# Two gate chunks of a fused encoder layer computed as a block product, and attention A's transposes and values one step later

## The chip, the cores and the metric

The kernel runs on one core of one Trainium2 chip. The metric is the device time of one execution in microseconds (us). A core has five engines with a queue each: TensorE (PE in the profile; its weight loads are shown as PEld), VectorE (DVE), ScalarE (ACT), GpSimd (POOL) and SyncE (SP), which here only issues transfers. Transfers run on 16 DMA engines that all queues share. An engine works through its queue in order, and waits there until what the next instruction needs is ready.

## The reference

One layer of an encoder is applied to two sequences, of 256 and 1024 rows of 1024 numbers, in float32. The kernel treats them as one matrix of T = 1280 rows, in three column blocks of 512, 512 and 256 when it is transposed.

```python
h = _rmsnorm(x, g_mix)
z = h @ w_in                      # queries, keys, values of branches A and B, and 2 x 1024 gates
...
gates = jax.nn.sigmoid((z[..., o6:] + b_gate).astype(jnp.float32)).astype(x.dtype)
gates = gates.reshape(b, S, 2, D_MODEL)
o_a, _ = _banded_attention(qa, ka, va, A_WINDOW, 1, rel_bias[:, :A_HEADS], sink)
o_b = _dilated_mixture(qb, kb, vb, rel_bias[:, A_HEADS:])
merged = gates[:, :, 0] * (o_a.reshape(b, S, A_Q) @ w_branch_a) + gates[:, :, 1] * (o_b @ w_branch_b)
x = x + merged @ w_out
h = _rmsnorm(x, g_mlp)
return x + jnp.square(jax.nn.relu(h @ w_up)) @ w_down
```

Attention A has 8 heads of 64 with 2 key heads, a window of 128 rows to either side, a bias by distance and a sink. Branch B has three groups of 4 heads, with windows that skip rows; their results are mixed by softmax weights. A final norm ends the layer.

## The kernel before

Every float32 matrix product is three matmuls on a rounded high part and the remainder (`mm3`, `six`): low by high, high by low, high by high. ScalarE makes the high part, VectorE the remainder.

**The input projection** produces 128 columns of z at a time, a *chunk*. The 16 gate chunks are c = 0 to 15. Most chunks are computed two at a time by `pair`, as a 2 x 2 block product of the 1024 long rows with seven block multiplications in place of eight (`seven`, each 12 matmuls of 512 columns), and two ordinary products for the 256 short rows (`prompt`, each 24 matmuls of 256 columns). `PAIRS` lists the pairs. The first `MIXED` of them run alone; beside the last five runs attention B (`attention_b`), advanced by a `tick`. The gates of a pair go to DRAM, `scr_g`, at once.

**Attention A** follows. `PLAIN` lists the gate chunks that no pair has; the generator `logits` computes them in the ordinary way (per chunk 48 matmuls of 512 columns and 24 of 256), as a *filler* that is advanced a few matmuls at a time: a group is four matmuls of 512 columns or eight of 256. A chunk has 15 groups. When a block is finished, ScalarE copies it to "gs", and SP stores it to `scr_g`.

A's main loop goes over n = 40 units of work, `order[j]` = (u, t), for u in 4 pairs of heads and t in 10 row tiles, two of them in one step (j = 0, 2, ..., 38). A step issues, in this order: the values of the step before last, the transposes of the last step, the scores of its own two tiles with filler between and behind them, their exponentials, two pieces of `merge` (which combines the three groups of B on POOL, with loads on SP), and loads that are due. `scores` takes two PSUM banks "sc", which VectorE frees when it has added the bias into the tile "s". `transposes` turns "s" in PSUM ("pt" and one "mm" bank) and copies it out with ScalarE and VectorE. `values_of` multiplies by v, copies to "o" on VectorE and stores it to `scr_o` on SP. A step transposes up to 12 blocks of 128 x 128, in three groups of four: the first and third group are copied by ScalarE, the second by VectorE. `values_of` needs all three.

**The gate jobs** come last: 24 for branch b, 24 for branch a. Job i multiplies a weight by a merged attention output, and VectorE multiplies the result by the opened gate into mT. Gates are loaded by `load_gate` (two gates share a slot "sg"), opened by a sigmoid in `open_gate` two jobs ahead, and requested eight jobs ahead. Before and beside the jobs the attention outputs are split in two parts: `high_b` and `low_b` for branch B, `turn_a` and `low_a` for A, after A's outputs have been divided by their row sums. The row sums are finished in `sums_a`, turned and written to DRAM in `rows_a`, and loaded back, spread over partitions, by `widen` ("wl").

From the first attention on, every engine's instructions stay in the order in which the program issues them. Tiles come from pools with a fixed number of slots: `slot` (33 of 4 KB per partition), `wslot` (10), `qslot` (8 of 1 KB), the attention pool (`a3`), and eight PSUM banks ("mm" 3, "sc" 2, "pt" 2, "pv" 1). A new tile waits until a slot of its pool is free.

Of the kernel before, what the change touches and what calls it, by code (L numbers as in the profile page):

```python
# [15 lines left out]
P = 128  # L16
# [30 lines left out]
PAIRS += [(0, P), (2 * P, 3 * P), (512, OFF_G)] + [(OFF_G + P * c, OFF_G + P * c + P) for c in (1, 3, 5, 7, 9)]  # L47

MIXED = 9
PLAIN = range(11, 16)  # L50
# [47 lines left out]
def encoder_kernel(  # L98
# [1046 lines left out]
    if True:  # L1145
# [14 lines left out]
        def scores(u, t):  # L1160
            st, bias = units[u]
            lo, W, c0 = tiles[t]
            s = a3("s", n=3)
            m = small.tile([P, 2], F32, name="m", tag="m")
            for h in range(2):
                ps = bank("sc")
                q = st["q"][h][:, P * t : P * t + P]
                nc.tensor.matmul(ps[:, :W], q, st["k"][1][:, P * lo : P * lo + W], start=True, stop=False)
                nc.tensor.matmul(ps[:, :W], q, st["k"][0][:, P * lo : P * lo + W], start=False, stop=True)
                nc.vector.tensor_tensor_reduce(  # L1170
                    s[:, h, :W], ps[:, :W], bias[:, h, c0 : c0 + W], 1.0, -3.0e38,
                    op0=ALU.add, op1=ALU.max, accum_out=m[:, h : h + 1],
                )
            nc.vector.scalar_tensor_tensor(nm_a[:, 2 * u : 2 * u + 2, t], m, -1.0, nsink[:, 2 * u : 2 * u + 2],
                                           op0=ALU.mult, op1=ALU.min)
            live[u, t] = s
# [22 lines left out]
        def values_of(u, t):  # L1199
# [12 lines left out]
            o = a3("o", (P, 2, P), 3)  # L1212
# [3 lines left out]
        def logits():  # L1216

            for i, c in enumerate(PLAIN):
                hi, lo = weight(0)
                for t0, n in BLOCKS[::2] + BLOCKS[1:2]:  # L1220
                    if i + 1 < len(PLAIN) and t0 == 0:
                        fetch()
                    ps = bank("mm")
                    yield from mm3(ps[:, :n], [((hi[:, k, :], lo[:, k, :]), h_at(k, t0, n)) for k in range(KC)],
                                   4 if n == 512 else 8)
                    z = wslot("gs", (P, 512))
                    nc.scalar.activation(z[:, :n], ps[:, :n], AF.Copy)
                    nc.sync.dma_start(scr_g[c][:, t0 : t0 + n], z[:, :n])
                    if i + 1 < len(PLAIN) and t0 == NS:
                        prepare()  # L1230
# [137 lines left out]
    if True:  # L1368
# [46 lines left out]
        def rows_a():  # L1415
# [3 lines left out]
            rows = a3("o", (P, 2, P), 3)[:n, 0, :]  # L1419
# [45 lines left out]
        for j in range(0, n + 2, 2):  # L1465
            if j > 2:
                values_of(*order[j - 4])
            if j:
                transposes(*order[j - 2])
            if j == n:  # L1470
                sums_a()
            if j < n:
# [5 lines left out]
                steps_of(fill, 2)  # L1478
# [4 lines left out]
            else:  # L1483
                steps_of(fill, 2)
                next(merges, None)
            if j == n - 4:
# [5 lines left out]
            if j in (n - 6, n - 4):  # L1492
                fetch()
            if j in (n - 4, n - 2):
                load_gate(j - n + 4)
                load_gate(j - n + 5)
                load_o(j - n + 4)
        prepare()
        values_of(*order[n - 2])
        run(merges)  # L1500
        next(fill)
        prepare()
        w_bs = [weight(0), weight(0)]
        w_as = [None] * 4

        rows_a()
        widen(0)
        fetch()
        for i in range(4):
            if i < 2:  # L1510
                open_gate(i)
            next(fill)
            if i == 0:
                high_b(1)
                low_b(1)
                widen(2)
        run(fill)
        for i in range(4, 8):
            load_gate(i)
        side = {0: [(weigh, 0)], 3: [(turn_a, 0)], 4: [(low_a, 0)], 5: [(turn_a, 1)], 6: [(low_a, 1)],  # L1520
# [6 lines left out]
        for i, (x, b, c) in enumerate(jobs):  # L1527
            t0, n = BLOCKS[b]
            load_gate(i + 8)
# [533 lines left out]
```

## Time and profile before

| what | value |
|---|---|
| median of three runs | 1672.1 us (1670.92 to 1672.12) |
| the profiled execution | 1671.05 us |
| its span, first to last instruction | 1669.3 us |
| granted TensorE clock | 0.999 |
| input pairs without attention beside them | 118.9 to 342.4 us |
| pairs beside attention B | 342.4 to 534.4 us |
| attention A with the filler | 534.4 to 681.0 us |
| gate jobs of branch b | 681.0 to 710.5 us |

A timeline row has the start and the length in us (of all its instructions, where several are merged), the engine, the line of the kernel, the operation, the output and the inputs, their sizes, the count, and in brackets the idle time of the engine before it with what ended it. A matmul's length overlaps with the next one's; what it costs is the distance between two starts. A row of a stretch has its limits and length, the busy time of each engine with its number of instructions, the granted clock, the busy share of the DMA engines, and the data rate. "SPq" is SP issuing transfers.

### The profile page before, as it was taken

How to read it: one execution, taken by the hardware profiler on the slowest of the kernel's cores; microseconds unless marked ns; L12 is line 12 of the kernel's file. 1: busy time of each engine (PE TensorE's matmuls, PEld its weight loads, DVE VectorE, ACT ScalarE, POOL GpSimd, SP SyncE). 2: the span in 40 equal slices, each digit the busy share in tenths (PEclk: the TensorE clock that was granted, in tenths of full speed). 3: DMA queues.
4: the chain of work that ended last, by engine and by line, in shares of the span. 5: the costliest groups of instructions: out<-in, count | busy, mean ns of one | idle time of the engine just before them, and what ended most of it. 6: DMA issues, size and time to landing. Idle time of an engine off the chain costs nothing.

```text
span 1669.3 us, 24690 instructions
## 1 busy us (share of the span) xinstructions
PE 1658.3 (99%) x9217; PEld 1410.3 (84%) x9217; DVE 954.1 (57%) x1535; ACT 715.1 (43%) x1473; POOL 484.8 (29%) x362
## 2 busy tenths in 40 slices
PE   9999999999999999999999999999999999999998
PEld 7898888888888888788888888888888888888886
DVE  6732233455654565677378455455456775867665
ACT  6232323345654565654176333333334333333435
POOL 1212222121112353000100555455554250514240
PEclk9999999999999999999999999999999999999999
DMA  7416562666667795965111443343356934733333
GB/s 257 150 53 127 135 126 78 169 185 200 187 192 220 196 236 162 254 203 202 46 81 59 161 161 125 117 161 130 113 191 235 359 115 136 253 102 108 120 121 126
DMA packets 226993, 265.11 MB, mean 159 GB/s; under 512 B 29663, under 2 KB 156511, under 8 KB 226873
## 3 DMA queue, kind: packets, MB, share of 16 engines
q1 hardware_dynamic: 219816, 245.35, 46.5%
q0 software_dynamic: 6720, 17.65, 5.3%
q8 instruction: 73, 1.20, 0.3%
q10 hardware_dynamic: 336, 0.53, 0.1%
q14 instruction: 48, 0.39, 0.1%
HBM read 177.75 MB, written 90.96 MB: 161 GB/s over the span
## 4 chain that ended last, share of the span: by engine, by line
PE 95%; DVE 2%; ACT 1%; DMA 1%; issue 0%; SPq 0%; ACTq 0%
PE dn L346 22%; PE x L346 20%; PE mm L192 13%; PE z L346 10%; PE v L820 6%; PE y L346 5%; PE mm L346 5%; PE sc L346 3%; PE pv L346 3%; PE pv L1210 2%; PE pt L1194 2%; PE sc L554 1%; PE pv L601 1%; PE pt L587 1%; PE tr L337 1%; DMA sg<-scr_g 1%
## 5 line engine op out<-in xcount | busy, mean ns | idle before, releaser
L346 PE MATMUL dn<-dhi,ulo 128*128 128x512 f32 x448 | 174.3, 389 | 0.0
L346 PE MATMUL dn<-dlo,uhi 128*128 128x512 f32 x448 | 174.3, 389 | 0.0
L346 PE MATMUL dn<-dhi,uhi 128*128 128x512 f32 x448 | 174.3, 389 | 0.0
L346 PE MATMUL x<-chi,wlo 128*128 128x512 f32 x424 | 166.5, 393 | 0.0
L346 PE MATMUL x<-clo,whi 128*128 128x512 f32 x424 | 165.6, 390 | 0.0
L346 PE MATMUL x<-chi,whi 128*128 128x512 f32 x424 | 165.0, 389 | 0.0
L313 DVE TENSOR_TENSOR wlo<-ta,whi 128x1024 fp32r<-128x1024 f32 x30 | 55.7, 1855 | 173.4 <-ACT whi L311 173.4
L392 POOL TENSOR_TENSOR tb<-raw 128x512 f32<-128x512 f32 x25 | 32.7, 1307 | 410.6 <-PE mm L192 159.2
L313 DVE TENSOR_TENSOR wlo<-raw,whi 128x1024 fp32r<-128x1024 f32 x60 | 89.7, 1496 | 103.7 <-ACT whi L311 101.0
L346 PEld LDWEIGHTS dn<-dlo,uhi 128*128 128x128 f32 x448 | 84.1, 188 | 17.5
L346 PEld LDWEIGHTS dn<-dhi,uhi 128*128 128x128 f32 x448 | 84.1, 188 | 17.4
L346 PEld LDWEIGHTS dn<-dhi,ulo 128*128 128x128 f32 x448 | 84.1, 188 | 17.3
L346 PEld LDWEIGHTS x<-chi,whi 128*128 128x128 f32 x424 | 79.6, 188 | 16.9
L346 PEld LDWEIGHTS x<-chi,wlo 128*128 128x128 f32 x424 | 79.8, 188 | 15.2
L346 PEld LDWEIGHTS x<-clo,whi 128*128 128x128 f32 x424 | 79.8, 188 | 14.6
L1755 POOL TENSOR_TENSOR t<-raw,t 128x1024 f32<-128x1024 f32 x16 | 45.7, 2870 | 148.6 <-DMA raw<-in_w_down_dram 148.5
L186 DVE TENSOR_TENSOR ulo<-uraw,uhi 128x1024 fp32r<-128x1024 f32 x56 | 86.1, 1558 | 4.5 <-ACT uhi L185 4.5
L1906 DVE TENSOR_TENSOR v<-v,dn 128x512 f32<-128x512 f32 x90 | 59.7, 683 | 40.5 <-PE dn L346 38.5
L2006 POOL TENSOR_TENSOR u<-u,u 128x640 f32<-128x640 f32 x16 | 25.1, 1570 | 179.0 <-ACT u L1924 179.0
L186 DVE TENSOR_TENSOR dlo<-raw,dhi 128x1024 fp32r<-128x1024 f32 x32 | 50.5, 1601 | 45.2 <-ACT dhi L185 44.2
L346 PE MATMUL dn<-dhi,up 128*128 128x512 f32 x224 | 73.5, 389 | 0.0
L346 PE MATMUL z<-chi,wlo 128*128 128x512 f32 x184 | 71.6, 389 | 0.0
(319 smaller groups left out, 4605.3 us busy)
## 6 DMA issues: line engine op xcount, KB each, us to landing
scr_u<-u SPq DMA_DIRECT2D x112, 320.0 KB, 2.6
uraw<-scr_u SPq DMA_DIRECT2D x56, 512.0 KB, 4.4
raw<-in_w_down_dram SPq DMA_DIRECT2D x36, 512.0 KB, 7.0
raw<-in_w_up_dram SPq DMA_DIRECT2D x32, 512.0 KB, 5.5
raw<-in_w_in_dram SPq DMA_DIRECT2D x25, 512.0 KB, 5.4
sg<-scr_g SPq DMA_DIRECT2D x32, 256.0 KB, 5.9
uraw<-scr_u SPq DMA_DIRECT2D x28, 256.0 KB, 4.4
qk<-scr_kb SPq DMA_DIRECT2D x48, 128.0 KB, 2.8
```

The costliest lines, as they stand in the source:

```text
L186: nc.vector.tensor_tensor(lo, src, hi.bitcast(F32), op=ALU.subtract)
L192: nc.tensor.matmul(ps, a, b, start=i == 0, stop=i == len(seq) - 1)
L313: nc.vector.tensor_tensor(lo, src, hi.bitcast(F32), op=ALU.subtract)
L337: nc.tensor.transpose(ps[:, P * i : P * (i + 1)], xn[t][:, P * k : P * (k + 1)], ident)
L346: nc.tensor.matmul(ps, a, b, start=first and i == 0, stop=last and i == len(seq) - 1, skip_group_check=True)
L392: (nc.vector if vector else nc.gpsimd).tensor_tensor(o, x, y, op=ALU.subtract)
L820: nc.tensor.matmul(ps[:, :n], a, b, start=k == 0 and j == 0, stop=k == KC - 1 and j == 2)
L1194: nc.tensor.transpose(ps[:, P * k : P * k + P], s[:, h, P * b : P * b + P], ident)
L1210: nc.tensor.matmul(pv[HALVES[h], P * i : P * i + P], src, pt[:, at + 2 * b + h, :], start=b == 0, stop=b == W // P - 1, skip_group_check=True)
L1755: nc.gpsimd.tensor_tensor(o, a, b, op=ALU.subtract)
L1906: nc.vector.tensor_tensor(v, v, ps, op=ALU.add)
L2006: nc.gpsimd.tensor_tensor(u[S1], u21, u22, op=ALU.add)
```

## The change

- Gate chunks 11 and 12 leave `PLAIN` and become a fifteenth pair. Ten pairs run alone, five beside attention B.
- In A's loop the transposes are issued two steps after their scores and the values three, each one step later than before. The loop has one step more at its end. "s" has four slots. "o" moves to `qslot`.
- The filler has 45 groups in place of 75. A step issues two of them in place of three. The last chunk computes its blocks in the order 0, 1, 2.
- Gates of jobs 0 to 11 are requested in steps n-4, n-2 and n, four in each; the jobs request twelve ahead. Before, gates 0 to 3 were requested in steps n-4 and n-2, and 4 to 7 after the filler.
- Weights of branch b are fetched in steps n-8 and n-6 and split in steps n-4 and n-2. `high_b(0)` and `low_b(0)` move from step n-4 to n-2. Opening the first two gates moves into step n, `rows_a` and the first `widen` to step n+2.
- The values of the last two tiles move beside job 1, as an entry `1: [(lambda last: values_of(*last), order[n - 2])]` of the table `side`.

```diff
-PAIRS += [(0, P), (2 * P, 3 * P), (512, OFF_G)] + [(OFF_G + P * c, OFF_G + P * c + P) for c in (1, 3, 5, 7, 9)]
+PAIRS += [(0, P), (2 * P, 3 * P), (512, OFF_G)] + [(OFF_G + P * c, OFF_G + P * c + P) for c in (1, 3, 5, 7, 9, 11)]
-MIXED = 9
-PLAIN = range(11, 16)
+MIXED = 10
+PLAIN = range(13, 16)
...
-            s = a3("s", n=3)
+            s = a3("s", n=4)
...
-            o = a3("o", (P, 2, P), 3)
+            o = qslot("o", (P, 2, P))
...
-                for t0, n in BLOCKS[::2] + BLOCKS[1:2]:
+                for t0, n in BLOCKS[::2] + BLOCKS[1:2] if i + 1 < len(PLAIN) else BLOCKS:
...
-            rows = a3("o", (P, 2, P), 3)[:n, 0, :]
+            rows = qslot("o", (P, 2, P))[:n, 0, :]
...
-        for j in range(0, n + 2, 2):
+        for j in range(0, n + 4, 2):
+            if j > 4:
+                values_of(*order[j - 6])
             if j > 2:
-                values_of(*order[j - 4])
-            if j:
-                transposes(*order[j - 2])
+                transposes(*order[j - 4])
             if j == n:
                 sums_a()
             if j < n:
...
                 scores(*order[j + 1])
-                steps_of(fill, 2)
+                next(fill, None)
...
-            else:
-                steps_of(fill, 2)
-                next(merges, None)
-            if j == n - 4:
+            if j == n - 2:
                 high_b(0)
                 low_b(0)
...
-            if j in (n - 6, n - 4):
+            if j in (n - 8, n - 6):
                 fetch()
             if j in (n - 4, n - 2):
-                load_gate(j - n + 4)
-                load_gate(j - n + 5)
+                prepare()
+            if j == n:
+                w_bs = [weight(0), weight(0)]
+                fetch()
+                next(merges, None)
+                steps_of(fill, 2)
+                for i in range(2):
+                    open_gate(i)
+            if j == n + 2:
+                rows_a()
+                widen(0)
+            if n - 6 < j < n + 2:
+                for i in range(4):
+                    load_gate(2 * (j - n + 4) + i)
+            if j in (n - 4, n - 2):
                 load_o(j - n + 4)
-        prepare()
-        values_of(*order[n - 2])
         run(merges)
-        next(fill)
-        prepare()
-        w_bs = [weight(0), weight(0)]
         w_as = [None] * 4
-
-        rows_a()
-        widen(0)
-        fetch()
-        for i in range(4):
-            if i < 2:
-                open_gate(i)
-            next(fill)
-            if i == 0:
-                high_b(1)
-                low_b(1)
-                widen(2)
+        high_b(1)
+        low_b(1)
+        widen(2)
         run(fill)
-        for i in range(4, 8):
-            load_gate(i)
...
-            load_gate(i + 8)
+            load_gate(i + 12)
```

More of the change, by code (lines that the diff above doesn't have):

```diff
@@ L1491, in encoder_kernel @@
                 units[u] = load_unit(u), load_bias(u, lambda name, shape: a3(name, shape, 2))
-            if j in (n - 6, n - 4):
+            if j in (n - 8, n - 6):
                 fetch()
             if j in (n - 4, n - 2):
-                load_gate(j - n + 4)
-                load_gate(j - n + 5)
+                prepare()
[13 more added lines that the diff above has]
+            if j in (n - 4, n - 2):
                 load_o(j - n + 4)
-        prepare()
-        values_of(*order[n - 2])
         run(merges)
-        next(fill)
-        prepare()
-        w_bs = [weight(0), weight(0)]
         w_as = [None] * 4
-        rows_a()
-        widen(0)
-        fetch()
-        for i in range(4):
-            if i < 2:
-                open_gate(i)
-            next(fill)
-            if i == 0:
-                high_b(1)
-                low_b(1)
-                widen(2)
+        high_b(1)
+        low_b(1)
+        widen(2)
         run(fill)
-        for i in range(4, 8):
-            load_gate(i)
-        side = {0: [(weigh, 0)], 3: [(turn_a, 0)], 4: [(low_a, 0)], 5: [(turn_a, 1)], 6: [(low_a, 1)],
+        side = {0: [(weigh, 0)], 1: [(lambda last: values_of(*last), order[n - 2])], 3: [(turn_a, 0)], 4: [(low_a, 0)], 5: [(turn_a, 1)], 6: [(low_a, 1)],
                 7: [(turn_a, 2)], 8: [(low_a, 2)], 9: [(turn_a, 3)], 10: [(low_a, 3)], 11: [(high_b, 2), (low_b, 2)],
```

## The prediction

> **What bounds the kernel now.** I read the page first, then the stretches of the two stages that trade work, then the timelines of their engines. The page says how full each engine is:
>
> ```profile
> span 1669.3 us, 24690 instructions
> ...
> PE 1658.3 (99%) x9217; PEld 1410.3 (84%) x9217; DVE 954.1 (57%) x1535; ACT 715.1 (43%) x1473; POOL 484.8 (29%) x362
> ```
>
> TensorE is idle for 11.0 us in all, so a change gains by issuing fewer matmuls or by closing one of the few holes. The stretches (length, then busy us of PE, PEld, DVE, ACT, POOL, granted clock, DMA share, GB/s) are a pair product without attention beside it, attention A with its filler, and the first 24 gate jobs:
>
> ```profile
> 317.61:342.45 24.84, 24.84 (x134) 21.52 (x133) 10.65 (x11) 8.22 (x12) 6.06 (x4) 1.00 0.66 172
> 534.40:681.03 146.63, 146.63 (x1149) 126.89 (x1148) 85.59 (x269) 84.77 (x225) 57.21 (x64) 1.00 0.73 198
> 681.03:710.50 29.47, 27.98 (x142) 23.27 (x141) 23.25 (x44) 19.67 (x38) 0.00 (x0) 1.00 1.06 295
> ```
>
> A has no TensorE idle time at all; the gate jobs have 1.49 us, with DMA full (1.06). The clock is 1.00 throughout.
>
> **The matmul sum.** A plain chunk is one 256-column block and two 512-column blocks of 24 matmuls. The last chunk's end in the TensorE timeline gives both prices (first matmul of the 256 block, first of a 512 block, first of the gate jobs):
>
> ```profile
> 672.69 0.28 PE L192 MATMUL mm<-phi,wlo 128*128 128x256 f32 x1
> ...
> 675.56 0.40 PE L192 MATMUL mm<-hhi,wlo 128*128 128x512 f32 x1
> ...
> 681.03 0.39 PE L192 MATMUL mm<-obhi,wlo 128*128 128x512 f32 x1
> ```
>
> 675.56 - 672.69 = 2.87 us and 681.03 - 675.56 = 5.47 us, so a chunk is 2 x 5.47 + 2.87 = 13.81 us and two leave A: -27.62 us. The pair product that replaces them runs as tenth unmixed pair, like the stretch at 317.61 that already writes a gate: +24.84 us. Net **-2.78 us**. Its ACT (8.22 us) and DVE (10.65 us) lie beneath 24.84 us of PE; its weights and stores ask for a DMA share near 0.66. Attention B still runs beside five pairs, with the same ticks, one pair later: nothing.
>
> **The later transposes and values.** These are the same instructions, one step further behind the scores. They need a fourth "s"; its room comes from "o", which goes to the q slots, three of which stay free while two units hold query tails, as many as "o" had. PE has no idle time before these instructions now, so the delay gains nothing by itself; it has to hold with 8 filler matmuls per step where there were 12 (0.228 us each, so 0.92 less). In the step quoted below the last exponentials have ended by 659.14 and the next transposes start at 660.50: 1.36 us of margin, of which the old order would lose 0.92. The new order adds a whole step to it. I count zero. The weights of b are requested one step earlier, the gates and heads by the same SP queue; SP's wait for a head's copy moves with the values.
>
> **The gate requests.** Two holes in the gate jobs come from the end of DVE's queue (mT frees the bank); for the second, ACT and SP show why:
>
> ```profile
> 685.66 0.50 PE L192 MATMUL mm<-obhi,wlo 128*128 128x512 f32 x1 [0.39 <-DVE mT L1551]
> ...
> 701.90 0.39 PE L192 MATMUL mm<-obhi,whi 128*128 128x512 f32 x1
> 703.39 0.50 PE L192 MATMUL mm<-obhi,wlo 128*128 128x512 f32 x1 [1.09 <-DVE mT L1551]
> ```
> ```profile
> 699.80 0.72 ACT L1454 ACTIVATE sg<-sg,bg 128x512 f32<-128x512 f32 x1 [1.75 <-DMA sg<-scr_g]
> ```
> ```profile
> 677.81 4.36 SPq L1228 DMA_DIRECT2D scr_g<-gs  x3
> 682.26 4.99 SPq L1449 DMA_DIRECT2D sg<-scr_g  x8
> ```
> ```profile
> 701.50 1.23 DVE L235 TENSOR_TENSOR wlo<-raw,whi 128x1024 fp32r<-128x1024 f32 x1 [2.06 <-ACT whi L231]
> ```
>
> SP stands behind the last chunk's stores until 682.2, then asks for eight gates at once; with DMA full one lands 1.75 us late, ACT opens it late, splits a weight late, and DVE's mT stands behind that split. Twelve gates asked for before that point take 1 MB out of the full stretch (four more gates of 256 KB; 295 GB/s, so 3.5 us of DMA). I count the second hole as closed: **-1.26 us** (701.90, the matmul before it, to 703.39, less 0.23).
>
> **What comes in place: DVE and ACT at A's end.** ACT and DVE run in program order. Today one 1024-wide split stands in a late step (obhi at n-4) with 12 fillers above it; the change puts one in n-4 (a weight), two in n-2 (obhi, a weight), and leaves 8 fillers. The nearest rows are that step:
>
> ```profile
> 656.63 0.28 PE L1168 MATMUL sc<-kk,q 128*128 128x256 f32 x1
> 659.04 1.53 PE L1210 MATMUL pv<-pt,va 128*64 128x128 f32 x24
> 660.50 1.31 PE L1194 MATMUL pt<-ident,s 128*128 128x128 f32 x10
> 661.57 0.36 PE L1168 MATMUL sc<-kp,qp 128*128 128x256 f32 x1
> ```
> ```profile
> 658.14 0.51 ACT L1180 ACTIVATE s<-s,nm_a 128x256 f32<-128x256 f32 x1
> 659.14 1.04 ACT L1378 ACTIVATE obhi<-merged 128x1024 fp32r<-128x1024 f32 x1
> ```
> ```profile
> 660.21 1.23 DVE L1381 TENSOR_TENSOR oblo<-merged,obhi 128x1024 fp32r<-128x1024 f32 x1 [2.17 <-ACT obhi L1378]
> 661.35 0.42 DVE L1213 COPY o<-pv 128x256 f32<-128x256 f32 x1
> 661.69 0.68 DVE L272 COPY pt<-pt 128x512 f32<-128x512 f32 x1
> 662.28 0.41 DVE L1170 CUSTOM_DVE_ANT_0 s<-sc,bias 128x256 f32<-128x256 f32 x1
> ```
>
> From the step's second scores (656.63) to the split is 2.51 us, the DVE half starts 1.07 later, then o copy +1.14, pt copy +0.34, biased scores +0.59. The next step's values stand 2.41 us after those scores today, behind eight fillers; behind four (4 x 0.228 less) it is 1.5. Values take 1.46, ten transposes 1.07 (twelve 1.28), four scores of 256 columns 0.5 (4 x 2.87 / 24).
> - Step n-2, from its values: split at 1.0, DVE half 2.1, o copy 3.2, pt copy 3.6, biased scores at 4.2, their first bank free near 4.6. PE wants that bank at 4.2 (1.46 + 1.28 + 0.5 + 0.92). It loses about **0.4 us**.
> - Step n: obhi at 1.0, the weight at 2.0; DVE's halves 2.1 and 3.2, o copy 4.4, pt copy 4.7 to 5.4. PE wants that copy for the values after 1.46 + 1.07 + 1.9 of filler (16 x 0.12), at 4.5. Half of the values' first tile may go ahead of it, so it loses 0.6 to 0.9; I take **0.75 us**.
>
> Then the gate jobs. Sigmoid's table load and the row sums' way through DRAM are:
>
> ```profile
> 670.98 1.28 ACT L1454 ACT_TABLE_LOAD   x1
> ```
> ```profile
> 672.96 0.33 SPq L1422 DMA_DIRECT2D scr_l<-o  x1
> 674.50 1.24 SPq L1431 DMA_DIRECT2D wl<-scr_l  x2
> ```
> ```profile
> wl<-scr_l SPq DMA_DIRECT2D x2, 256.0 KB, 4.3
> ```
> ```profile
> DMA to landing us min/median/max: 3.7/7.2/9.4
> ```
>
> The last two rows are the landings of the first two wl transfers and of all ten. On step n's clock (0 at its values; 512-wide passes of 0.5 on ACT and 0.68 on DVE, as the pt copies) ACT does: sums 5.8, gate store copy 6.35, table load to 7.6, two gates (at most 0.72 each, the row at 699.80) to 8.9, pt copy 9.4, obhi(1) 10.35, the short gate copy 10.65, gate three 11.3, weight a(0) 12.25; DVE its half to 13.45 and the first mT to 14.1. PE, which today has the last chunk's filler here (672.69 to 681.03), starts job 0 at 8.6, values of the last heads 10.0, jobs 1 and 2 to 13.75, and wants that bank: **0.4 us**, in place of today's 0.55 hole of the same kind (685.66). The row sums leave SP near 9.3, come back as wl issues from 10.8 to 12.0, (1.54 after the store, 1.24 long) and land 4.3 us after issue, near 16.2; turn_a(0) ends at 16.9, the mT behind it at 17.6, and job 6 wants it at 18.3. So wl is now just in time where it was long there. With a landing of 7.2 us (its median over all ten) job 6 waits about 2.2 us: that is the upper bound.
>
> **Sum.** -2.78 - 1.26 - 0.55 + 0.4 + 0.75 + 0.4 = -3.04. Against the profiled execution (1671.05 us, of which the span is 1669.3): 1668.0. The median of the three runs is 1.05 us above it, 1672.1, so I forecast **1669.1**.
>
> **Earlier in A: margins, no cost.** By step u=3's start, A runs 16.3 us earlier (15 steps x 0.93, and one step's values and transposes, 2.4). What it needs:
>
> ```profile
> 612.27 0.87 SPq L433 DMA_DIRECT2D q<-scr_qa  x2
> ```
> ```profile
> 613.73 0.74 POOL L453 DMA_DIRECT2D bias<-wide  x1
> ```
> ```profile
> 634.59 0.36 PE L1168 MATMUL sc<-kk,q 128*128 128x256 f32 x1
> ```
> ```profile
> DMA to landing us min/median/max: 3.8/7.8/8.8
> ```
> ```profile
> 600.00:620.00 20.00, 20.00 (x168) 17.57 (x166) 13.16 (x36) 11.40 (x33) 14.61 (x11) 1.00 0.98 255
> ```
>
> The last bias lands by 613.73 + 8.8 = 622.5 and is wanted at 618.7 (634.59 - 16.3, + 0.4 for scores). Its request stands behind the merge's products on POOL, and those behind DMA that is nearly full. The merge's products start earlier too, by 8.0 us (6 x 0.93 + 2.4), so I take it as in time.
>
> **Rivals.**
> - *The late splits cost nothing* (a copy is read by parts, or ACT is earlier): both A waits and the job wait vanish, -2.78 - 1.26 - 0.55 = -4.6, 1667.5. For: nearest rows show today's split passing without a PE wait. Against: they have four more fillers above it. Chance 0.38, from -3.4 on.
> - *Slower: the DMA-bound merge keeps its old times.* Then the bias or q is late by up to 622.5 - 618.7 = 3.8 us, and wl, behind the gates in a full DMA, holds job 6 by 2.2: -3.04 + 6.0 = +3.0, 1675.1. It costs once less than 3.8 us of the merge's head start arrive, and makes the kernel slower than before from 3.04 us of such waits. For: the share of 0.98. Against: A's fill asks for 1/3 less, and SP's head start. Chance 0.12, a third of it beyond 0.2%.
> - *A does not shrink.* If steps kept 6.9 us, 20 steps lose nothing, the pair's 24.84 stays and only 10 of the filler's groups of four matmuls go (13 stand behind the loop's last scores today, 3 after; 0.93 each): +15.5 us. Its point is a chain of scores, exponentials and transposes longer than two new steps, 12.2 us; from 656.63 by way of the split's start at 659.14 to 660.50 it is 3.9. Chance 0.03.
>
> [...]
>
> **Chances.** A measurement of this kernel can tell 0.2%, 3.3 us, from no change. Forecast 0.47; first rival 0.38, second 0.12, third 0.03. My forecast sits just inside 0.2%, so a little of it falls beyond: faster 0.42, same 0.51, slower 0.07 (the third rival and a third of the second). The range goes from the first rival with 0.3 to spare (1667.2) to the forecast with wl late and the bias a little (1672.8).
>
> **What would show it.** Right: a tenth unmixed pair of 24.84 us; A with its filler near 120 us; no wait on sg near job 13; waits of 0.4 to 0.8 us on DVE copies in the last two steps. Wrong: TensorE idle at the start of u=3, mT behind wl at job 3, steps of 6.9 us.

## The result, and the profile after

The changed kernel takes 1679.27 us (median of 8 runs, 1676.85 to 1683.64), the kernel before 1672.18 us (8 runs beside them). The ratio is 1.0038, with a 95% interval of 1.0025 to 1.0051: slower by 7.1 us, where 3.0 us less were forecast. The profiled execution has a span of 1677.7 us against 1669.3.

The page's first lines:

```profile
span 1677.7 us, 24632 instructions
...
PE 1659.5 (99%) x9205; PEld 1410.6 (84%) x9205; DVE 957.7 (57%) x1540; ACT 716.0 (43%) x1475; POOL 491.3 (29%) x366
```

TensorE is idle for 18.2 us, 7.2 more than before. The stretches that answer to those of before are the tenth unmixed pair, A with its filler, and the gate jobs of branch b (columns as in the prediction):

```profile
342.40:367.24 24.84, 24.84 (x135) 21.52 (x134) 6.93 (x7) 6.95 (x10) 9.56 (x8) 1.00 0.53 149
559.38:684.79 125.41, 120.44 (x989) 104.39 (x988) 80.93 (x265) 77.84 (x214) 56.82 (x64) 0.97 0.82 215
684.79:719.33 34.54, 30.27 (x163) 24.43 (x162) 25.05 (x48) 21.77 (x44) 0.00 (x0) 1.00 0.94 270
```

The pair is there. A has become 21.2 us shorter (146.59 to 125.41) where the forecast's terms come to 27.5, and its granted clock is 0.97. The gate jobs have become 4.7 us longer (29.87 to 34.54). The pairs end 24.94 us later and the rest after these jobs is 0.03 us shorter, so 24.94 - 21.18 + 4.67 - 0.03 = +8.4 us, the difference of the spans.

**A's loss** is one place, the first step of the third pair of heads (u = 2). TensorE's timeline, then ACT's, POOL's and DVE's:

```profile
624.09 1.09 PE L1210 MATMUL pv<-pt,vp 128*64 128x128 f32 x16
625.12 1.31 PE L1194 MATMUL pt<-ident,s 128*128 128x128 f32 x10
630.70 0.69 PE L1168 MATMUL sc<-kk,q 128*128 128x384 f32 x1 [4.27 <-DVE m L1170]
...
632.14 0.63 PE L192 MATMUL mm<-hhi,whi 128*128 128x512 f32 x1
632.57 0.63 PE L192 MATMUL mm<-hhi,wlo 128*128 128x512 f32 x1
```
```profile
625.02 0.38 ACT L1227 ACTIVATE gs<-mm 128x256 f32<-128x256 f32 x1 [3.94 <-DMA r<-scr_b]
627.85 1.06 ACT L231 ACTIVATE whi<-raw 128x1024 fp32r<-128x1024 f32 x1 [2.44 <-DMA r<-scr_b]
```
```profile
610.79 1.28 POOL L1342 TENSOR_TENSOR merged<-r 128x512 f32<-128x512 f32 x1 [14.06 <-DMA r<-scr_c]
...
623.46 1.53 POOL L1345 TENSOR_TENSOR merged<-merged,r 128x512 f32<-128x512 f32 x1
624.95 1.27 POOL L1342 TENSOR_TENSOR r<-r 128x512 f32<-128x512 f32 x1
626.30 1.52 POOL L1345 TENSOR_TENSOR merged<-merged,r 128x512 f32<-128x512 f32 x1
```
```profile
628.94 1.22 DVE L235 TENSOR_TENSOR wlo<-raw,whi 128x1024 fp32r<-128x1024 f32 x1 [5.54 <-ACT whi L231]
630.08 0.55 DVE L1170 CUSTOM_DVE_ANT_0 s<-sc,bias 128x384 f32<-128x384 f32 x1
```

TensorE waits for a bank "sc", which DVE frees with the biased scores at 630.08. Those stand behind the remainder of the last plain chunk's weight, which waits for ACT's high part at 627.85, and that stands behind the gate copy "gs". The bracket names a transfer into "r", the merge's tile, which neither of ACT's two instructions reads. But gs, whi and r all come from the ten `wslot` slots. gs starts at 625.02, as POOL's add of 623.46 ends (624.99); whi at 627.85, as the add of 626.30 ends (627.82). So each seems to wait for a slot that the merge still holds; the experiments test that. Behind the hole the matmuls of 512 columns start 0.43 us apart, not 0.23, and the clock's column (last but two) shows why:

```profile
617.00:624.00 7.00, 7.00 (x56) 5.98 (x54) 4.96 (x13) 3.00 (x9) 5.11 (x5) 1.00 0.95 212
624.00:631.00 7.00, 2.73 (x28) 2.23 (x28) 2.06 (x4) 2.64 (x6) 5.43 (x5) 0.84 0.90 229
631.00:637.00 6.00, 6.00 (x28) 5.11 (x29) 5.90 (x15) 3.36 (x10) 5.83 (x5) 0.62 0.86 221
```

The step lasts from 624.09 to 636.34, 12.25 us; the same step takes 5.87 us in e7_pace below, which has no hole there.

**The gate jobs' loss** is a row of holes. TensorE's, then the DVE and SP rows behind the large one:

```profile
690.75 0.50 PE L192 MATMUL mm<-obhi,wlo 128*128 128x512 f32 x1 [0.44 <-DVE mT L1545]
697.55 0.50 PE L192 MATMUL mm<-obhi,wlo 128*128 128x512 f32 x1 [2.38 <-DVE mT L1545]
...
713.62 0.39 PE L192 MATMUL mm<-obhi,wlo 128*128 128x256 f32 x1 [0.97 <-DVE mT L1545]
```
```profile
696.20 0.69 DVE L1395 TENSOR_TENSOR o<-o,wl 128x512 f32<-128x512 f32 x1 [3.98 <-DMA wl<-scr_l]
...
712.27 0.69 DVE L1395 TENSOR_TENSOR o<-o,wl 128x512 f32<-128x512 f32 x1 [1.44 <-DMA o<-scr_o]
```
```profile
683.37 1.92 SPq L1449 DMA_DIRECT2D sg<-scr_g  x4
685.38 0.38 SPq L1214 DMA_DIRECT2D scr_o<-o  x1
685.86 0.38 SPq L1422 DMA_DIRECT2D scr_l<-o  x1
690.91 2.59 SPq L1431 DMA_DIRECT2D wl<-scr_l  x4
```

The hole ahead of job 3 (0.44) is the forecast one. The one at job 6 is the row sums: their store went out at 685.86 behind four gates, and the wide sums ("wl", the row sums spread over partitions) could be requested only 5.05 us later, not 1.54 as before. The wait on a gate near job 13 is gone, but at job 17 DVE waits for o rows (A's outputs) instead.

### The profile page after: what moved, and what is told of

Its sections match the earlier page's. It is cut to its first block, busy times and chain, and to the rows that moved or that the text cites. A ratio compares the mean times of both kernels' runs of the same rounds, so it can differ in the third digit from the quotient of the medians.

```text
span 1677.7 us, 24632 instructions
## 1 busy us (share of the span) xinstructions
PE 1659.5 (99%) x9205; PEld 1410.6 (84%) x9205; DVE 957.7 (57%) x1540; ACT 716.0 (43%) x1475; POOL 491.3 (29%) x366
## 4 chain that ended last, share of the span: by engine, by line
PE 92%; DMA 2%; DVE 2%; ACT 2%; SPq 1%; issue 0%; ACTq 0%; DVEq 0%
PE dn L346 22%; PE x L346 20%; PE mm L192 11%; PE z L346 10%; PE v L820 6%; PE y L346 5%; PE mm L346 5%; PE sc L346 3%; PE pv L346 3%; PE sc L554 1%; PE pt L587 1%; PE pv L601 1%; PE pt L1194 1%; PE pv L1210 1%; PE tr L337 1%; PE sc L1168 1%
## 5 line engine op out<-in xcount | busy, mean ns | idle before, releaser
L346 PE MATMUL x<-chi,wlo 128*128 128x512 f32 x436 | 171.2, 393 | 0.0
L346 PE MATMUL x<-clo,whi 128*128 128x512 f32 x436 | 170.2, 390 | 0.0
L346 PE MATMUL x<-chi,whi 128*128 128x512 f32 x436 | 169.7, 389 | 0.0
```

The lines of the kernel that those rows point to most:

```text
L346: nc.tensor.matmul(ps, a, b, start=first and i == 0, stop=last and i == len(seq) - 1, skip_group_check=True)
```

## The experiments

Lengths are from the first matmul after the pairs to that of job 0 (A), and from there to the first of branch a (b jobs), in the profiled execution; the ratio is to the kernel before, run beside it. The kernel before had medians of 1670.88 to 1671.49 us beside the later runs, so rows are compared by their ratios. Four kernels with the same gate jobs (after, e1_pause, e7_pace, e5_slots) show 33.70 to 34.60 us for them: a difference below 1 us in one execution says little.

| run | A, us | b jobs, us | median, us | ratio [95%] |
|---|---|---|---|---|
| before | 146.59 | 29.87 | 1672.18 | 1 |
| after | 125.41 | 34.54 | 1679.27 | 1.0038 [1.0025, 1.0051] |
| e1_pause | 118.83 | 34.60 | 1672.28 | 1.0001 [0.9992, 1.0010] |
| e7_pace | 118.69 | 33.70 | 1672.39 | 1.0006 [0.9996, 1.0016] |
| e5_slots | 122.00 | 33.72 | 1676.19 | 1.0028 [1.0018, 1.0037] |
| e2_gates | 124.69 | 32.93 | 1677.83 | 1.0037 [1.0024, 1.0050] |
| e8_gates_o | 118.92 | 31.89 | 1671.18 | 0.9998 [0.9988, 1.0007] |
| e9_weigh | 118.80 | 32.24 | 1670.75 | 0.9997 [0.9988, 1.0005] |
| e4_nodelay | 127.88 | 30.16 | 1678.67 | 1.0047 [1.0034, 1.0061] |
| e10_eight | 118.40 | 35.83 | 1674.47 | 1.0016 [1.0007, 1.0025] |
| e11_early | 118.99 | 33.21 | 1672.35 | 1.0008 [0.9999, 1.0016] |
| e12_nowl | 119.31 | 29.47 | 1668.11 | 0.9982 [0.9972, 0.9992] |
| e13_wide | 120.39 | 31.15 | 1670.22 | 0.9997 [0.9988, 1.0006] |
| e14_before_wide | 146.40 | 28.42 | 1670.38 | 0.9995 [0.9986, 1.0004] |
| e15_apart | 120.45 | 32.56 | 1671.34 | 1.0001 [0.9992, 1.0010] |
| e16_copies | 119.40 | 39.31 | 1680.72 | 1.0052 [1.0038, 1.0065] |
| e17_one | 118.82 | 55.80 | 1711.86 | 1.0239 [1.0225, 1.0253] |
| e18_before_one | 146.93 | 60.91 | 1708.94 | 1.0229 [1.0214, 1.0243] |
| e19_both | 119.14 | 29.75 | 1668.06 | 0.9980 [0.9972, 0.9989] |
| e20_sixteen | 118.85 | 31.98 | 1672.19 | 1.0008 [0.9999, 1.0017] |

### Is the hole in A the merge's slots?

e1_pause lets the merge skip two steps, so that fewer of its tiles are held when gs and whi come:

```diff
-                if j > 2:
+                if j > 2 and j not in (12, 14):
                     steps_of(merges, 2)
```

> The merge of branch B skips two steps of A's loop (12 and 14), so its products and their loads come two steps later. Theory: in the changed kernel ScalarE's gate store copy and weight split at the start of u=2 wait 3.9 and 2.4 us for w slots that POOL's late products still hold; the DVE half of the split stands in front of the biased scores, and TensorE idles 4.3 us and then runs some us at a lower granted clock. With the products issued later in the program, POOL is less far behind it, and the wait falls below 1 us: about 6 us faster than the changed kernel (ratio to before near 1.000). Rival, the split waits for the weight's own DMA or for full DMA as such: the wait stays near 4 us, ratio 1.003 to 1.004.

e7_pace slows it to three pieces in two steps from step 14 on:

```diff
-                    steps_of(merges, 2)
+                    steps_of(merges, 2 if j < 14 or j % 4 else 1)
```

> The merge's 18 products are issued three per two steps in place of four. Theory of the held slots: less work in front of POOL per step, ScalarE's waits at u=2 shrink but the first products are as early as before, so 2 to 6 us are gained on the changed kernel (ratio to before 1.000 to 1.0025). Rival, full DMA as such: the same bytes per us up to u=2's start, no gain there (1.0035).

e5_slots gives only gs another pool:

```diff
-                    z = wslot("gs", (P, 512))
+                    z = slot("gs", (P, 512))
```

> The filler's store copies gs take m slots in place of w slots; pace and order of the merge stay. Theory of the held slots: gs no longer waits (3.9 us less on ScalarE); the weight split still shares the w slots with the products, with one or two more free, so the 4.3 us hole on TensorE shrinks by at least 3 us, ratio to before 1.000 to 1.002. Rival, full DMA or POOL's own lateness delays TensorE by another way: the hole stays.

Both paces take the hole away, and A is 118.8 and 118.7 us long. In e7_pace ACT's rows have no wait in brackets any more:

```profile
620.73 0.37 ACT L1227 ACTIVATE gs<-mm 128x256 f32<-128x256 f32 x1
620.99 1.05 ACT L231 ACTIVATE whi<-raw 128x1024 fp32r<-128x1024 f32 x1
```

By the ratios (1.0038 and 1.0001) the whole kernel gains 6.2 us by e1_pause, about A's 6.6. Another slot for gs alone gives 3.4 us of A, and a ratio above the one expected: gs and whi wait no more, but the remainder, next in need of a slot, waits for POOL's add by name (e5_slots, DVE):

```profile
623.71 2.30 DVE L235 TENSOR_TENSOR wlo<-raw,whi 128x1024 fp32r<-128x1024 f32 x1 [1.58 <-POOL merged L1345]
```

So the merge's hold on the slots is the cause, and not the transfers for the units of heads, which ask for the same in e1_pause as in the changed kernel.

### Is the extra step of delay needed?

e4_nodelay is e8_gates_o (below) with the transposes one step after the scores and the values two, as before:

```diff
-            if j > 4:
-                values_of(*order[j - 6])
-            if j > 2:
-                transposes(*order[j - 4])
+            if 2 < j < n + 2:
+                values_of(*order[j - 4])
+            if 0 < j < n + 2:
+                transposes(*order[j - 2])
```

> As e8_gates_o, but transposes follow one step after their scores and values two, as before the change; all else stays. Theory: with 8 filler matmuls per step the exponentials of a step end 0.4 us before its transposes are due or after them, so TensorE waits in most full steps, 0 to 0.7 us each: A is 3 to 10 us longer than e8_gates_o (122 to 129 us), ratio 0.9985 to 1.004. Rival: the delay was not needed, A stays at 118.7 to 119.5 us.

A becomes 9 us longer than in e8_gates_o. The rows of the transposes among A's groups show part of it; the last columns are the idle time before them and what ended it. First e4_nodelay, with the turning of the row sums at A's end, then e8_gates_o:

```profile
L1194 PE MATMUL pt<-ident,s 128*128 128x128 f32 x208 | 29.7, 281 | 3.6 <-ACT s L1180 3.5
...
L1418 PE MATMUL tn<-ident,l_a 128*80 128x128 f32 x1 | 0.4, 407 | 2.6 <-DVE l_a L1413 2.6
```
```profile
L1194 PE MATMUL pt<-ident,s 128*128 128x128 f32 x208 | 27.0, 278 | 0.0
```

With two groups of filler a step, the exponentials (ACT L1180) come too late for transposes one step behind: 3.5 us of idle time. Another 2.6 us is the row sums, which then wait for DVE. What the remaining 3 us are stays open. The delay is not a gain of its own; it is what makes the smaller filler possible.

### What bounds the gate jobs?

e2_gates requests gates 8 to 11 behind the wide row sums, not ahead of their store:

```diff
-            if n - 6 < j < n + 2:
+            if n - 6 < j < n:
...
         widen(2)
+        for i in range(8, 12):
+            load_gate(i)
```

> Gates 8 to 11 are requested behind wl instead of ahead of the row sums' store. Theory: that store takes 5.1 us to land (1.5 before) since four gates of 256 KB stand ahead of it, and DVE then waits 4.0 us for wl in front of job 3's mT, so job 6 loses 2.4 us; without them the store lands in 1.5 to 2.5 us and the hole before job 6 falls below 0.5 us: 2.0 to 2.4 us faster than the changed kernel, ratio to before 1.0024. Rival, wl itself is slow with DMA full of gates 0 to 7: the hole stays over 1.5 us.

e8_gates_o adds the pace of e7_pace and asks for o rows 4 in job 1, not 7; e9_weigh then moves a weight split from job 0 to job 2:

```diff
-        side_loads = {5: [(widen, 4)], 7: [(load_o, 4)], 10: [(widen, 6)], 12: [(load_o, 6)],
+        side_loads = {1: [(load_o, 4)], 5: [(widen, 4)], 10: [(widen, 6)], 12: [(load_o, 6)],
```
```diff
-        side = {0: [(weigh, 0)], 1: [(lambda last: values_of(*last), order[n - 2])], 3: [(turn_a, 0)], 4: [(low_a, 0)], 5: [(turn_a, 1)], 6: [(low_a, 1)],
+        side = {1: [(lambda last: values_of(*last), order[n - 2])], 2: [(weigh, 0)], 3: [(turn_a, 0)], 4: [(low_a, 0)], 5: [(turn_a, 1)], 6: [(low_a, 1)],
```

> Three edits on the changed kernel: the merge at three products per two steps, gates 8 to 11 requested behind wl, A's outputs of rows 4 and 5 requested in job 1 in place of job 7. Theory: the loop's hole at u=2 (6 us with the slow clock), the hole before job 6 (2.4) and the one near job 18 (1.0 to 2.0, VectorE waiting for those outputs, which land 8 to 10 us after a request among the gates) go; A is 118.7 us long, the jobs of branch b 30.5 to 31.2 (27.5 of matmuls, 1.0 of values, the 0.45 hole before job 3, some weight switches), and the kernel is 5 us faster than before: ratio 0.9965 to 0.998. Rival, DMA is simply full from 680 to 715 and a hole only moves to whatever stands last: jobs over 32 us, ratio 0.9985 to 1.000.

> As e8_gates_o, and the split of branch a's first weight moves from job 0 to job 2, out of the way of the first mT on VectorE. Theory: the 0.45 us hole before job 3 is VectorE's weight split (1.2 us) in front of mT; it goes, 0.3 to 0.5 us faster than e8_gates_o (ratio 0.0003 lower, not to be told apart by times; by the hole in the trace). Rival: the split only stands before another mT, and the same hole opens before job 5 or 6.

Each edit closes the hole that it is aimed at, and another opens. In e2_gates the store of the row sums has no gates ahead of it, and the wide sums are requested 2.24 us behind it:

```profile
684.23 0.33 SPq L1422 DMA_DIRECT2D scr_l<-o  x1
686.47 2.57 SPq L1431 DMA_DIRECT2D wl<-scr_l  x4
```

The hole at job 6 is gone, but 2.05 us open at job 17, and the ratio stays (1.0037 against 1.0038, where 1.0024 was expected). e8_gates_o has the ratio of its rival. e9_weigh has no hole at jobs 3 and 6, and this one, behind a weight of branch a that comes late (TensorE, then ACT):

```profile
702.40 0.50 PE L192 MATMUL mm<-obhi,wlo 128*128 128x512 f32 x1 [2.37 <-DVE mT L1547]
```
```profile
699.43 1.06 ACT L231 ACTIVATE whi<-raw 128x1024 fp32r<-128x1024 f32 x1 [2.33 <-DMA raw<-in_w_branch_a_dram]
```

e10_eight is e9_weigh without early requests of gates 8 to 11, and with eight ahead in the jobs. e11_early is e9_weigh with o rows 4 and the third pair of wide sums requested ahead of those gates. First the edit of e10_eight in the jobs, then that of e11_early:

```diff
-            load_gate(i + 12)
+            load_gate(i + 8)
```
```diff
         widen(2)
+        load_o(4)
+        widen(4)
         for i in range(8, 12):
             load_gate(i)
...
-        side_loads = {1: [(load_o, 4)], 5: [(widen, 4)], 10: [(widen, 6)], 12: [(load_o, 6)],
+        side_loads = {4: [(load_o, 6)], 7: [(widen, 6)],
```

> Undoes the part 'twelve gates among A's last heads': four are requested at step n-4 and four at step n-2, the jobs request eight ahead as before the change; slower merge, weight split in job 2 and o-rows 4 in job 1 as in e9_weigh. Theory (in the gate jobs the 16 DMA engines are full, so the order of requests only moves the hole; the twelve early requests are worth little): the b jobs take 31 to 33 us again, with 1.5 to 3 us of TensorE holes in all, ratio 0.998 to 1.001. Rival (early requests fill DMA time that is free in A's last steps, so four fewer cost their transfers' time): four gates of 256 KB at the 0.38 MB per us of these jobs are about 2.7 us later, b jobs 34 to 35, ratio 1.001 or more.

> What else is due in the jobs is requested ahead of gates 8 to 11: behind the wide row sums of rows 2 to 3 come o-rows 4, the wide row sums of rows 4 to 5, then the four gates; o-rows 6 and the next wide sums follow in jobs 4 and 7; slower merge and weight split in job 2 as in e9_weigh. Theory (DMA full: the hole moves to whichever request stands last): the hole of 2.4 us at job 13 goes or shrinks, and one of 1 to 3 us shows on gates 8 to 11 (jobs 8 to 13) instead; b jobs 31 to 33 us, ratio 0.998 to 1.001. Rival (only the order was wrong): holes under 0.5 us in all, b jobs 30.0 to 30.5 us, ratio 0.997 to 0.9985.

In e10_eight my theory falls and the rival holds: four fewer early requests cost 3.6 us of b jobs (32.24 to 35.83). 1.9 us of it are holes (4.63 against 2.69 us); most of the rest is a granted clock of 0.58 from 704.6 to 709.0 us, behind the last hole. Asking early is worth its transfers. In e11_early the hole has moved to 697.37 (2.58 us), as the theory has it; order alone doesn't remove it.

e12_nowl leaves eight of the ten transfers of wide sums away:

```diff
+            if t:
+                wide_l[t // 2] = wide_l[0]
+                return
             r = wide_l[t // 2] = slot("wl", (P, 4, 2 * P))
```

> Leaves out eight of the ten transfers that bring the wide row sums (256 KB each, 2 MB in all, six of the eight within the b jobs): the first rows' sums serve for all rows. Otherwise e9_weigh. Theory (DMA bounds the b jobs): with 1.5 MB of about 9 MB gone from them, no TensorE hole over 0.6 us is left there, b jobs 29.8 to 30.5 us against 32.2 in e9_weigh, ratio 0.997 to 0.9985. Rival (the holes come from ACT and VectorE behind their own queues, not from transfers): b jobs stay at 31.5 us or more with a hole of 1.5 us or more, ratio 0.999 to 1.0005.

No idle time of 0.15 us or more is left before any matmul of the b jobs, which take 29.47 us, and the kernel is faster than before. ACT's wait for the weight is gone too. So transfers bound the gate jobs, and the wide sums are the load that tips it. The row of the stretch 694 to 704 us (the last two columns are DMA share and GB/s) in e9_weigh and in e12_nowl:

```profile
694.00:704.00 10.00, 7.63 (x34) 6.01 (x33) 6.20 (x11) 5.16 (x9) 0.00 (x0) 1.00 0.98 241
```
```profile
694.00:704.00 10.00, 9.92 (x50) 8.02 (x49) 9.06 (x17) 7.04 (x15) 0.00 (x0) 1.00 0.98 328
```

The DMA engines are as busy with 241 GB/s as with 328. Bytes of wide sums cost more than other bytes.

### Why are the wide sums dear?

Small pieces? e13_wide keeps the row sums in another order, so that a partition reads one piece of 4 KB, not four of 1 KB; e14_before_wide is the kernel before with that edit. The reading side:

```diff
-                nc.sync.dma_start(r[HALVES[h]], bass.AP(a.tensor, a.offset + T * h + P * t, [[0, HD], [2 * T, 4], [1, 2 * P]]))
+                nc.sync.dma_start(r[HALVES[h]].rearrange("p u q -> p (u q)"),
+                                  bass.AP(a.tensor, a.offset + 4 * T * h + 4 * P * t, [[0, HD], [1, 8 * P]]))
```

> e9_weigh with one more edit: the row sums are kept in the order (head of the pair, pair of row blocks, unit, row block), so that a transfer of the wide row sums reads 4 KB in one piece for each partition instead of four pieces of 1 KB; bytes and everything else unchanged. Theory (DMA bounds the gate jobs, and the ten transfers of the wide sums are dear in it because of their small pieces: in the trace of e9_weigh the rate is about 0.22 MB per us in the stretches where they run and about 0.38 where gates run): six of them fall in the b jobs and would take about 0.65 us each instead of 1.2, some 3 us of the engines' time less; no hole over 0.6 us there, b jobs 29.5 to 30.3 us against 32.2, ratio 0.9975 to 0.999, faster than before. Rival (the slow stretches are slow for another reason, such as four gates being issued behind them on one queue): rate and holes as in e9_weigh, b jobs 32 us, ratio 0.999 to 1.0005.

> The kernel before the change with the same edit alone (wide row sums read in pieces of 4 KB). It tells what the edit is worth without the change. If the DMA engines bound the gate jobs only with the change: b jobs stay near 29.9 us, the two gate holes ahead of job 0 may lose some tenths, ratio 0.9985 to 1.0005, and e13_wide is the faster one by 0.1% or more. If the edit does for before what it does for the changed kernel: ratio 0.998 or less, and the change is worth nothing beside it.

A hole of 1.77 us stays at 703.43 in e13_wide, behind the same weight: piece size isn't the main reason. In e14_before_wide the holes of the b jobs are gone (28.42 us), but the ratio's interval holds 1; what the edit is worth to the kernel before stays open at this size.

One address for 64 readers? e15_apart reads attention rows, an address for each partition, in two transfers of 64 partitions as before. e19_both reads the same rows in one transfer of 128 partitions:

```diff
+            if t == 0:
...
+                return
             for h in range(2):
-                nc.sync.dma_start(r[HALVES[h]], bass.AP(a.tensor, a.offset + T * h + P * t, [[0, HD], [2 * T, 4], [1, 2 * P]]))
+                nc.sync.dma_start(r[HALVES[h]].rearrange("p u (i q) -> p u i q", q=P), scr_o[0][HALVES[h]])
```
```diff
-            for h in range(2):
-                nc.sync.dma_start(r[HALVES[h]].rearrange("p u (i q) -> p u i q", q=P), scr_o[0][HALVES[h]])
+            nc.sync.dma_start(r.rearrange("p u (i q) -> p u i q", q=P), scr_o[0])
```

> e9_weigh, but eight of the ten transfers of the wide row sums read 256 KB of attention rows instead, each partition at an address of its own, where the kernel reads one and the same 4 KB for 64 partitions; bytes, order and waits on the queue as before. Leaves the row sums of all but the first rows out of the result. Theory (64 readers of one address are what makes these transfers slow): the rate rises from about 0.22 to 0.35 MB per us or more in the stretches where they run, b jobs 29.5 to 30.3 us without a hole over 0.6 us, as in e12_nowl, ratio 0.9975 to 0.999. Rival (the bytes and the place in the queue cost it, whatever is read): rate and hole as in e9_weigh, b jobs 31.2 to 32.3 us, ratio 0.999 to 1.0005.

> e15_apart with the two transfers of 256 KB into 64 partitions joined into one of 512 KB into all 128 (of attention rows in place of the row sums, 128 addresses, the same kind of transfer as that of the o rows). Leaves the row sums of all but the first rows out of the result. Theory (a transfer into half of the partitions goes at half the rate): 694 to 704 us rises from 0.28 MB per us to 0.34 or more, no hole over 0.6 us, b jobs 29.5 to 30.3 us, ratio 0.9975 to 0.999. Rival (the bytes alone): a hole of 1.5 us or more as in e15_apart, b jobs 31 us or more, ratio 0.999 to 1.001. e17_one's loss had another reason: its outermost dimension is 2, and the DMA share was 0.13, two engines of sixteen, where that transfer ran alone.

The issue rows have the size and the median time to landing; below each, the stretch 694 to 704 us. e15_apart:

```profile
wl<-scr_o SPq DMA_DIRECT2D x8, 256.0 KB, 7.8
```
```profile
694.00:704.00 10.00, 8.03 (x36) 6.35 (x35) 7.02 (x12) 6.14 (x11) 0.00 (x0) 1.00 1.06 282
```

And e19_both:

```profile
wl<-scr_o SPq DMA_DIRECT2D x4, 512.0 KB, 5.5
```
```profile
694.00:704.00 10.00, 9.59 (x47) 7.69 (x47) 8.48 (x16) 7.08 (x14) 0.00 (x0) 1.00 0.97 326
```

The same bytes from the same place: in halves a hole of 1.98 us stays, whole there is one of 0.41. ACT's wait for the weight of branch a, 1.93 us in e15_apart, is 0.47 in e19_both. The b jobs are 2.8 us shorter (about 1.3 of it a drop of the clock, last section), and the kernel is faster than before. The address of the readers changes little (273 GB/s in e13_wide, 282 in e15_apart), the half of the partitions more (282 against 326). Half the rate, which the theories of e19_both and e17_one assume, is not shown: other transfers run in that stretch too. The two runs also differ in the number of transfers, eight against four, which no run varies alone; against that as the cause stands the DMA share, 1.06 with the lower rate: the engines were busy, not short of requests.

Why it costs more is not shown. Four kernels tried to make the wide sums cheaper with every row sum in its place. e16_copies stores the sums eight times and lets eight partitions read each copy, still in halves. e17_one reads both halves in one transfer, and e18_before_one does so in the kernel before. e20_sixteen stores sixteen pieces and reads them in one transfer. Their reading sides, in the order e16_copies, e17_one (with e18_before_one), e20_sixteen, in place of e13_wide's:

```diff
-[[0, HD], [1, 8 * P]]
+[[0, 8], [AH * T, 8], [1, 8 * P]]
+[[4 * T, 2], [0, HD], [1, 8 * P]]
+[[4 * T, 16], [0, 8], [1, 8 * P]]
```

> e13_wide with the row sums stored eight times (320 KB instead of 40), and each copy read by 8 of the 64 partitions. Result complete. Theory (readers of one address): with an eighth of the readers for each address the wide sums go at 0.3 MB per us or more, b jobs 29.8 to 30.8 us, ratio 0.9975 to 0.9992; the store lands up to 1 us later, and some of that may show at job 6. Rival (bytes alone): 0.28 MB more to move, 0.7 us at 0.38, so b jobs 31.5 us or more and ratio 1.000 to 1.001.

> e13_wide with one transfer of 512 KB into all 128 partitions for each pair of row blocks, in place of two of 256 KB into 64 partitions each. Theory (a transfer into half of the partitions goes at half the rate, whatever its pieces and whatever it reads): the stretches at about 0.22 MB per us rise to 0.35 or more, no hole over 0.6 us in the gate jobs, b jobs 29.5 to 30.3 us, ratio 0.9975 to 0.999, faster than before. Rival (the bytes alone, or requests on one queue): rate and hole as in e13_wide, b jobs 31 to 32.3 us, ratio 0.999 to 1.0005.

> The kernel before the change with the same edit alone: row sums in the new order, one transfer of 512 KB for each pair of row blocks. If half the partitions were the reason: b jobs 28.4 us as in e14_before_wide (that kernel had no hole left in them, so no more is to be gained there), the gate holes ahead of job 0 unchanged or some tenths smaller, ratio 0.9985 to 1.0. What e17_one is below this one is what the change is worth where the transfers don't bound the jobs: about 1 us if A's gain stands.

e16_copies is 0.5% slower than before, beyond its theory and its rival, and the other two over 2%. In e17_one the first wide sums are requested at 680.72; from 682 to 688 us hardly anything else moves, and then TensorE stands idle for 7.69 us until 695.64:

```profile
682.00:688.00 6.00, 5.96 (x27) 4.59 (x25) 3.23 (x5) 2.28 (x4) 0.00 (x0) 1.00 0.13 45
```

A share of 0.13 is 2 of 16 engines (2/16 = 0.125), and 2 is the outermost dimension of the source. That the one sets the other is my reading of this row. By it these two runs say nothing of the halves, and e16_copies, with 8 outermost, may be spoilt in the same way: its share is 0.54 from 684 to 688 us, behind the request of its first wide sums. In e20_sixteen 16 stands outermost:

> e13_wide with the row sums stored as sixteen pieces of memory, eight copies for each head of a pair (320 KB), and one transfer of 512 KB for each pair of row blocks whose outermost dimension is 16, eight partitions each, into all 128 partitions. Result complete. Theory (the outermost dimension sets how many of the 16 engines carry a transfer, 2 in e17_one and 8 in e16_copies): no stretch at a DMA share of 0.13, the four-fold loss of e17_one is gone; with half the partitions as the reason also, b jobs 29.6 to 30.6 us and ratio 0.9975 to 0.9992, faster than before. If only the first holds and not the second: b jobs 31 to 32.5 us, ratio 0.999 to 1.001. If neither: ratio over 1.004 as in e16_copies.

The loss of e17_one is gone: the DMA share is 1.09 from 694 to 704 us, with wide sums requested at 694.79 and 700.23, where e17_one has 0.57 (695.6 to 700 us) and 0.26 (700 to 704 us). But the b jobs take 31.98 us, with a hole of 1.47 us at 702.50, and the ratio is 1.0008. That is its middle case: the half of the partitions is not shown to be the whole reason with the row sums themselves. It differs from e19_both in that eight partitions share an address, in its outermost dimension (16, not 128), and in 0.28 MB more stored; which of these matters was not tried. No complete version that beats the kernel before was found: e9_weigh, e13_wide and e14_before_wide are level with the kernel before.

## Why the prediction was wrong

**The matmul sum held.** The pair costs 24.94 us (24.84 forecast), and A without the hole is 118.7 to 118.9 us long (e1_pause, e7_pace, e8_gates_o, e9_weigh), where the terms give 146.59 - 27.62 - 1.03 (values moved into the jobs) + 1.15 = 119.1. In e19_both, where neither loss is left, the span is 2.7 us below the span before; -3.04 was forecast. As that kernel leaves most row sums out and asks for its transfers in another order, the agreement is no test of the sum. From -3.04 to the +8.4 us of the spans it is 11.4 us: 6.3 in A (125.41 against 119.1), 5.05 in the gate jobs, 0.1 in the pair.

**"Earlier in A: margins, no cost" failed: +6.6 us.** I took the merge's products to start 8.0 us earlier with the program. Before, the first load and POOL's first product were these, and the first load of the changed kernel the last row:

```profile
579.08 0.42 SPq L1323 DMA_DIRECT2D r<-scr_b  x1
```
```profile
589.18 1.29 POOL L1342 TENSOR_TENSOR merged<-r 128x512 f32<-128x512 f32 x1 [10.56 <-DMA r<-scr_c]
```
```profile
597.38 1.15 SPq L1323 DMA_DIRECT2D r<-scr_b  x1
```

589.18 + 24.84 - 8.0 = 606.0; it came at 610.79, so 3.2 us of the 8.0 arrived. The load was asked for 6.5 us earlier (579.08 + 24.84 - 597.38), but from there to the product it took 3.3 us longer (13.41 against 10.10): the merge is held by its transfers (DMA share 1.02 from 600 to 617 us). That is the slower rival's mechanism, which I gave a chance of 0.12. But I looked for its price only at the tiles that the merge's transfers delay (bias, q), which cost nothing. The price fell on a pool of slots that the merge shares with the filler, one pair of heads earlier, through ACT's and DVE's order: 4.3 us of idle time and some 2.1 us more in the rest of that step, at the lower clock.

**"The gate requests" failed: the b jobs gain no 1.26 us, and 3.8 us come in addition.** The forecast makes them 29.87 - 1.26 - 0.55 + 0.4 + 1.03 = 29.49 us long; they are 34.54. The hole of 1.26 us did close, and the twelve early gates earn their transfers (e10_eight). But I counted what leaves the full stretch and not what enters it. Before, the row sums' turning stood 9.4 us ahead of job 0, with the last filler between; now it stands 1.1 us ahead (before, then the changed kernel), and four transfers of wide sums, 1 MB at a low rate (220 GB/s from 693 to 697.5 us, 388 from 697.5 to 701), fall into the jobs:

```profile
671.65 0.27 PE L1418 MATMUL tn<-ident,l_a 128*80 128x128 f32 x1
```
```profile
683.72 0.27 PE L1418 MATMUL tn<-ident,l_a 128*80 128x128 f32 x1
```

For job 6 I had taken 0, since I reckoned with the request 1.54 us after the store, where it took 5.05 behind the gates. The upper bound that I named, 2.2 us, is near the 2.38 found by luck: it stood for a slow landing of the wide sums, but they let DVE go on 5.29 us after their first request (690.91 to 696.20), where I had 5.4 (10.8 to 16.2). It was the store that was late.

**The waits at A's end.** For 0.4 us in step n-2 the changed kernel has 0.25 us of idle time, and the other runs with the delay 0.19 to 0.76, so the size was about right. The 0.75 us in step n were too much: no idle time of 0.15 us or more is there. The hole ahead of job 3 is 0.44 us where 0.4 was forecast. **The delay** does hold where it was needed, by e4_nodelay; "I count zero" was right for the exponentials.

## What to carry to other kernels

When a program moves earlier but its transfers don't, list every pool of slots that the late work shares with the early work, not only the tiles that arrive late; an in-order engine turns one missing slot into a hole elsewhere (here ACT's waits of 3.94 and 2.44 us became 4.27 us of TensorE). When a stretch is full of DMA, count both what leaves and what enters it, in engine time and not bytes: transfers into half of the partitions cost more here for each byte than those into all (282 against 326 GB/s in e15_apart and e19_both, at DMA shares of 1.06 and 0.97). Before you shape a transfer by hand, look at its outermost dimension: with 2 there the DMA share was 0.13 (e17_one, 682 to 688 us), with 16 it was 1.09 (e20_sixteen, 694 to 704 us).

## What the runs showed of the hardware

The granted clock drops behind some holes and not behind others. Behind 4.27 us it was 0.62, and behind 2.38 us (changed kernel) and 2.37 us (e9_weigh) it stayed at 1.00. But in e15_apart 1.98 us of idle time were followed by this, 3 us long, in which matmuls of 256 columns start 0.21 us apart, not 0.12:

```profile
701.00:704.00 3.00, 1.02 (x5) 0.56 (x4) 2.38 (x3) 1.60 (x3) 0.00 (x0) 1.00 1.05 228
704.00:707.00 3.00, 3.00 (x14) 2.73 (x14) 2.91 (x7) 1.92 (x5) 0.00 (x0) 0.63 0.97 217
```

The other runs show the same in A and the gate jobs of branch b. Ten holes there are 1.95 to 2.58 us long; a slow stretch of some 3 us or more follows five of them (1.95 in e7_pace, 1.98 in e15_apart, 1.99 in e10_eight, 2.27 in e5_slots, 2.58 in e4_nodelay) and none the other five (2.05 in e2_gates, 2.37 in e9_weigh, 2.38 in the changed kernel, 2.54 in e16_copies, 2.58 in e11_early). No hole of 1.77 us or less was followed by one, and each of 2.74 us or more was.

The length of the hole alone doesn't decide: behind 2.58 us the clock dropped in e4_nodelay and not in e11_early. What decides is not shown.
